# Scratch arrays of queries and keys laid out by plain rows instead of stacked blocks, in a hybrid encoder layer on one core

## The chip, the cores and the metric

The kernel runs on one core of a Trainium2 chip. The metric is the device time of one execution in microseconds (us), the median of several. In the profile PE is TensorE's matmuls, PEld its weight loads, DVE VectorE, ACT ScalarE, POOL GpSimd, SP SyncE, which here only issues DMAs; SPq and ACTq are the sequencers of SP and ACT, where a DMA's issue takes its time. L12 is line 12 of the kernel.

## The reference, cut to what matters

One encoder layer on x [2048, 1024], float32. Four token mixers read columns of one projection; the change touches the arrays of two of them, the differential attention (z_q, z_k) and the latent attention (from c_q, c_kv, k_r).

```python
a = rmsnorm(h, g_mix[i])
z = a @ w_in[i]
z_hy, z_s5, z_q, z_k, z_v, c_q, c_kv, k_r = split_mixer_columns(z)
y_hy = hyena_mixer(z_hy, ...); y_s5 = s5_mixer(z_s5, ...)
y_da = diff_attention(z_q..., z_k..., z_v..., lam, lam_init, da_g_head[i])   # 4 heads, 2 maps of 32
y_mla = mla_attention(c_q, c_kv, k_r, ...)     # 4 heads, 64 plain + 32 rotated; k_r shared by the heads
h = h + concatenate([norm(y_hy), norm(y_s5), y_da, norm(y_mla)]) @ w_out[i]
h = h + (silu(f @ w_gate[i]) * (f @ w_up[i])) @ w_down[i]      # f = rmsnorm(h)
h = h + sigmoid(rmsnorm(h) @ w_ple_gate[i]) * (p[i] @ w_ple[i])
return rmsnorm(h, g_final)
```

## The kernel before

Float32 products are made of fp32r ones: a number is split into hi + lo (`split`, `split_scaled`: ACT writes hi, DVE lo), and a product is three matmuls, hi hi, hi lo, lo hi (`mm3`, L52 to L54). The scores of attention do the same by stacking. For a differential map, 32 rows of a query's hi, hi, lo lie under each other on 96 partitions, against a key's hi, lo, hi, so that one matmul over 96 rows is the three products. For the latent attention, 64 plain rows and 32 rotated ones make 96, once for hi and once for lo, and a chunk of scores is three matmuls.

The stages, in the program's order:

1. *Input projection* (`InProj.run`), two halves of 1024 tokens. In each, groups of 256 or 304 columns: weights come by four loads (w_raw, L114, two places), are split, and products follow for two chunks of 512 tokens. Results go to scratch arrays in HBM. The columns of queries and keys pass through `to_stack` (L157): hi and lo tiles of [128, 512] (four blocks of 32 rows) are stored into S["qda"] and S["kda"], shaped [8, 96, 2048], hence each store names its target as 4 blocks x 32 rows x 512 tokens; one part is stored twice. These stores are issued on ACT's queue.
2. *Background.* Generators put their instructions between those of the foreground: first the Hyena filters, then `mla_prep`, which starts when the second half's latent columns are there; both must be through before attention. `mla_prep` runs over four chunks of 512 tokens: load c (L258), norm, rotate the shared key part, transpose (L291), project (L308), split into mp_hi and mp_lo (two places each), store to S["qml"] and S["kml"], shaped [4 heads, 2 parts, 96, 2048] (L319: 2 heads x 64 rows x 512; L331: 4 heads x 32 rows; L301: the rotated keys, the same rows for four heads, with the 32 rows outermost), then values: product, mp_v (one place), store of 128 rows (L339). Its PSUM tiles ps_hy have two places. All its DMAs, like the projection's weight loads, are on SP's queue, which issues in order.
3. *Attention* (`Attention`, `Unit`): per head 16 units of 128 queries, twelve chunks of scores each, the remaining background between them. Keys of a head are four tiles [96, 2048] with one place each (L368), asked for again when the last unit of a head has used them; a unit's queries are one tile [96, 4, 128] with two places, loaded by two DMAs (L409, L410).
4. Output projection, feed-forward part, gated embedding, final norm (L727 and on), which the change doesn't touch.

The order of instructions on each engine is set once, when the program is built, by a scheduler from the program's order and its priorities; on the chip each engine and each queue runs its list in order.

Of the kernel before, what the change touches and what calls it, by code (L numbers as in the profile page):

```python
# [24 lines left out]
class Ops:  # L25
    """Small helpers shared by the parts of the kernel."""
# [5 lines left out]
    def after(self, inst, earlier):  # L32
        """inst is issued after an earlier one of the same engine."""
        self.tc.add_manual_dep(inst.ins, earlier.ins.name, mybir.DependencyInfo(
            mybir.DependencyClass.NoSync, mybir.DependencyReason.DATA), reason="issue order")

    def split(self, hi, lo, src):
        """hi + lo == src exactly, each with 12 significant bits; src in SBUF or PSUM."""
        nc = self.nc
        nc.scalar.activation(hi, src, AF.Copy)  # L40
        nc.vector.tensor_sub(lo, src, hi.bitcast(F32))  # L41

    def split_scaled(self, hi, lo, src, scale):
        """The split of src * scale; scale is a number or one value per partition."""
        nc = self.nc
        nc.scalar.activation(hi, src, AF.Copy, scale=scale)
        nc.vector.scalar_tensor_tensor(lo, src, scale, hi.bitcast(F32), ALU.mult, ALU.subtract)

    def mm3(self, ps, lhs, rhs, first, last):
        """ps += lhs.T @ rhs, both given as (hi, lo)."""  # L50
# [5 lines left out]
    def rsqrt(self, y, v, t):  # L56
        """y = v ** -0.5 for v > 0, to float32's rounding; t is scratch. All [P, n]."""
# [8 lines left out]
def load_column(nc, dst, vec, n):  # L66
    """dst[p, c] = vec[c * 128 + p]"""
    nc.sync.dma_start(dst, vec.rearrange("(c p) -> p c", p=128))


class NormT:
    """Rows of a [SEQ, DM] stream -> rms norm -> transposed, scaled by g, split in two."""
# [5 lines left out]
    def chunk(self, rows, hi, lo, n=4, keep=False):  # L78
        """rows: n APs [128, DM] in SBUF, scaled in place unless kept; hi, lo: [128, 8, 128 n]."""
# [22 lines left out]
class InProj:  # L102
    """The columns of rmsnorm(x) @ w_in go to their scratch arrays."""
# [28 lines left out]
    def run(self, const, step, ready):  # L132
        """ready() comes when the latent attention's columns are there."""
        o, nc, A, S = self.o, self.nc, self.A, self.S
        with ExitStack() as ctx:
# [11 lines left out]
            def to_stack(dst, hi_rows, lo_row, scale):  # L147
                def done(ps, m, n0):
# [6 lines left out]
                    for src, rows in ((hi, hi_rows), (lo, (lo_row,))):  # L155
                        for r in rows:
                            nc.scalar.dma_start(dst[ds(4 * m, 4), ds(32 * r, 32), ds(n0, 512)], src.bitcast(F32))  # L157
                return done

            for half in range(2):  # L160
# [36 lines left out]
                columns_of((1024, to_stack(S["qda"], (0, 1), 2, qs)))  # L197
                columns_of((1280, to_stack(S["kda"], (0, 2), 1, None)))
# [10 lines left out]
                # chunk by chunk, so that the next half's first one finds a place early  # L209
# [15 lines left out]
def mla_prep(ops, const, A, S, cp, wk, ps_pool):  # L225
    """Queries, keys and values of the latent attention from the rows c_q | c_kv | k_rope.
    Queries carry minus the softmax scale; both come apart in two for the float32 products.
    A generator."""
# [26 lines left out]
    for ch in range(4):  # L255
# [44 lines left out]
        for j in range(2):  # L300
            nc.sync.dma_start(S["kml"][:, j, 64:96, ds(n0, 512)].rearrange("h d n -> d h n"),  # L301
                                a2[j][64:96].bitcast(F32)[:, None, :].to_broadcast([32, 4, 512]))
# [9 lines left out]
        for m in range(2):  # L312
            for dst, pairs, scale in ((S["qml"], q, MLA_SCALE), (S["kml"], ((wkv, kv),), 1.0)):
# [4 lines left out]
                for j, src in enumerate((hi, lo)):  # L318
                    nc.sync.dma_start(dst[ds(2 * m, 2), j, 0:64, ds(n0, 512)], src.bitcast(F32))  # L319
# [10 lines left out]
        for j, src in enumerate((hi, lo)):  # L330
            nc.sync.dma_start(S["qml"][:, j, 64:96, ds(n0, 512)], src.bitcast(F32))  # L331
# [11 lines left out]
class Attention:  # L343
    """Softmax attention over blocks of 128 queries, of a differential head (0) and a latent head (1) at a time.

    Scores lie as [query, key], with the sign changed, so that their least value is the maximum's
    negative; the weights are transposed on the tensor engine for the product with the values, and
    the sums' reciprocals scale the result."""

# [13 lines left out]
    def keys(self, i, h):  # L363
        """Two maps' keys of the differential head h, then two parts of the latent head's."""
        if h < 4:
            self.k[i] = self.kp.tile([96, SEQ], F32R, name=f"k{i}_sb")
            src = self.S["kda"][2 * h + i] if i < 2 else self.S["kml"][h, i - 2]
            self.nc.sync.dma_start(self.k[i].bitcast(F32), src)  # L368

    def values(self, i, h):  # L370
        """Half i of the keys' values."""
# [6 lines left out]
    def run(self, step):  # L378
        """One unit's chunks of scores at a time; after chunk k come the steps of PLAN[k], each of the unit so many
        units before."""  # L380
# [15 lines left out]
class Unit:  # L396
    """128 queries of two heads."""
# [6 lines left out]
    def chunk(self, k):  # L404
        at, nc, n = self.at, self.nc, self.t % 2
        if k == 0:
            tok = ds(128 * self.t, 128)
            self.q = at.qp.tile([96, 4, 128], F32R, name="q_sb")
            nc.sync.dma_start(self.q[:, 0:2].bitcast(F32), at.S["qda"][ds(2 * self.h, 2), :, tok].rearrange("m d n -> d m n"))  # L409
            nc.sync.dma_start(self.q[:, 2:4].bitcast(F32), at.S["qml"][self.h, :, :, tok].rearrange("j d n -> d j n"))  # L410
# [13 lines left out]
    def scores(self, name, c, products):  # L424
        """A chunk of scores, and of the last one the exponentials and their sum."""
# [20 lines left out]
    def combine(self):  # L446
        """The first map's weights less lambda times the second one's, times the first one's sum"""
# [15 lines left out]
    def scale(self, hd):  # L463
        """diag(1 / total)"""
# [20 lines left out]
    def weigh(self, piece):  # L485
        """The values' sums, by eight pieces of two chunks of keys, then times the queries' scales."""
# [25 lines left out]
def attention_consts(ops, cp, tmp, A):  # L512
    """strip[p, j] = |j - 1920 - p|, exact in 16 bits; neg_lam = minus the differential
    attention's lambda."""
# [20 lines left out]
def inverse_rms(ops, sm, rows, junk):  # L535
    """1 / the root mean square of each of some rows, a column each"""
# [9 lines left out]
class OutProj:  # L546
    """h = x + mix @ w_out with the branches' norms, and f = rmsnorm(h), transposed. The norms' gains go into w_out."""

    def __init__(self, st, const, A, S, cp):
# [11 lines left out]
        # columns that pick the two heads of 128 channels, or all of them  # L561
# [8 lines left out]
    def weights(self):  # L570
        """Forms the operands of w_out; those without a place yet go to scratch. A generator."""
# [9 lines left out]
    def fetch(self):  # L581
        """The operands that weights() put into scratch."""
# [5 lines left out]
    def prepare(self, t, wk, ps_pool):  # L588
        """mix of rows 256 t to 256 t + 255, transposed."""
# [6 lines left out]
        # mean squares: two branches' by row, four heads' and one branch's from their columns  # L596
# [17 lines left out]
        for m in range(2):  # L614
# [7 lines left out]
            # the columns' scales from diagonal matrices  # L622
# [14 lines left out]
    def run(self, wk, nwk, ps_pool, ps_norm):  # L637
        """Returns what is left to do: the last rows' norms."""
# [31 lines left out]
class Strassen:  # L670
    """C = A @ B by Winograd's seven products of blocks, A [256, K] and B [K, 1024] in 2 by 2 blocks:
    A11 B11, A12 B21, S4 B22, A22 T4, S1 T1, S2 T2, S3 T3 with S1 = A21 + A22, S2 = S1 - A11, S3 = A11 - A21,
    S4 = A12 - S2, T1 = B12 - B11, T2 = B22 - T1, T3 = B22 - B12 and T4 = B21 - T2 (its sign changed).
    Each product is one of float32 operands split in two."""
# [6 lines left out]
    def start(self, ctx):  # L681
        """The first pools, for four of B's operands and what they are formed from."""
# [5 lines left out]
    def complete(self, ctx):  # L688
        """The other pools, but those of raw() and sum()."""
        self.temporary.close()  # L690
        # what is needed first lies where attention's keys did, which are free before the rest
# [7 lines left out]
    def places(self, name, c, n=2):  # L699
        """An operand's tiles of chunks c and c + 1."""  # L700
# [7 lines left out]
    def forming(self, kb, load, scratch=None):  # L708
        """B's operands, with kb chunks of 128 rows in a block; load(tile, row of blocks, column, chunk) fills a
        tile with chunks from the given one on. The last three operands go to scratch, if given, by way of  # L710
        others' places. A generator."""
# [38 lines left out]
    def normed(self, dst, tok, h, g, const, wk, ps_pool, halves):  # L750
        """128 rows' norms times g, transposed; halves() gives the places of half of them as they are and transposed."""
# [14 lines left out]
    def halves(self):  # L766
        """Places for normed()."""
# [3 lines left out]
    def raw(self):  # L771
        """Tiles for two blocks of A, transposed: [row in a chunk, chunk, row of A]."""
        return [self.ar.tile([128, 4, 256], F32, name="a_raw") for _ in range(2)]

    def product(self, kb, raw, done):
        """done(row, column, terms) gets a block of C as the sum of terms, of which the first may lie in PSUM."""
# [49 lines left out]
    def sum(self, terms):  # L826
        """The sum, in SBUF or PSUM."""
# [10 lines left out]
def ffn(st, const, A, S, ctx, first):  # L838
    """h2 = h + (silu(f @ w_gate) * (f @ w_up)) @ w_down, from f transposed; first() follows the loads of the first
    half of f. Returns what is left to do: the norms of h2's last rows."""  # L840
    nc, last = st.nc, []
    # S["g"] = silu(f @ w_gate) * (f @ w_up), transposed
# [24 lines left out]
    # 6 or 8 chunks of the hidden columns at a time  # L867
# [40 lines left out]
def embedding(ops, const, A, S, cp, wk, ps_pool):  # L908
    """S["emb"] = p @ w_ple, 512 columns at a time. A generator."""
# [30 lines left out]
def ple(st, const, A, S, ctx, out, last):  # L940
    """out = rmsnorm(h2 + sigmoid(rmsnorm(h2) @ w_ple_gate) * emb); last is done first."""
# [46 lines left out]
def reduce_angle(nc, z, k):  # L988
    """z -= 2 pi * round(z / 2 pi), in place; k is scratch."""
# [8 lines left out]
class Dft16:  # L998
    """16-point complex transforms along the middle of z [128, 2 (re, im), 16, C], as two rounds of
# [826 lines left out]
```

## Time and profile before

| | us |
|---|---|
| runs | 4011.3, 4014.12, 4016.09; median 4014.12 |
| span of the profiled execution | 4006.2 |
| median less that span | 7.9 |
| TensorE busy over the span | 3526.0 (88%) |
| VectorE, ScalarE, GpSimd busy | 2700.0, 1801.4, 1863.9 |
| projection and preparation, until the first scores | 0 to 733.4 |
| attention, first to last score product | 733.4 to 2116.3 |

A busy share over the whole span mixes stages with different limits, so the stretches matter: in the page's 40 slices TensorE is busy seven to nine tenths and more in the last third, and five to six tenths in slices 5 to 8 (400 to 800 us). The profile keeps one time for the profiled execution, the span above; it is read beside the median.

### The profile page before, as it was taken

What the parts mean: (1) busy time and instruction counts of PE and PEld (TensorE: products, weight loads), DVE (VectorE), ACT (ScalarE), POOL (GpSimd) and SP (SyncE); (2) the same over time, 40 slices, a digit from 0 to 9 for tenths busy, and PEclk for the clock granted to TensorE, in tenths of its full rate; (3) what the DMA queues carried; (4) which work ended last, traced back from release to release, by engine and by line L of the source; (5) the groups of instructions that cost most, each with busy time, mean ns of one, the idle gap of its engine ahead of it and who ended that gap; (6) DMA issues with size and microseconds to landing.
All of it is one profiled execution on the core that took longest, in us unless ns stands there. A gap on an engine that the chain in (4) does not pass through costs nothing. (4 is left out here: it accounts for less than half of the span.)

```text
span 4006.2 us, 55513 instructions
## 1 busy us (share of the span) xinstructions
PE 3526.0 (88%) x19814; PEld 2806.2 (70%) x19814; DVE 2700.0 (67%) x5382; ACT 1801.4 (45%) x3089; POOL 1863.9 (47%) x1735
## 2 busy tenths in 40 slices
PE   8899656689999997877889879999999998989887
PEld 7789555466677775665667767888788876767666
DVE  6557322587776569888987786444845576768877
ACT  5224211366676765555565434333433343333344
POOL 1224000046419448767666655445544444344454
PEclk9999878799999998887998989999999999999988
DMA  4544432412442431241226453222322245544644
GB/s 144 177 140 163 141 112 87 108 50 82 152 153 82 130 132 54 74 130 41 62 82 216 137 158 118 84 82 84 107 88 74 85 138 172 178 168 153 206 153 156
DMA packets 349492, 486.18 MB, mean 121 GB/s; under 512 B 52987, under 2 KB 253439, under 8 KB 344703
## 3 DMA queue, kind: packets, MB, share of 16 engines
q1 hardware_dynamic: 273440, 370.69, 29.0%
q10 hardware_dynamic: 75776, 111.96, 8.0%
q8 instruction: 156, 2.56, 0.3%
q14 instruction: 120, 0.98, 0.1%
HBM read 313.46 MB, written 173.29 MB: 122 GB/s over the span
## 5 line engine op out<-in xcount | busy, mean ns | idle before, releaser
L434 PE MATMUL ps_s<-k_sb,q_sb 96*128 96x512 f32 x1280 | 474.8, 462 | 126.3 <-DVE four_s L439 52.7
L804 PE MATMUL ps_st<-t_hi,s_hi 128*128 128x512 f32 x984 | 398.3, 405 | 47.7 <-DVE st_sum L831 22.2
L444 ACT ACTIVATE at_s<-at_s,least_s 128x2048 f32<-128x2048 f32 x192 | 383.8, 2000 | 114.1 <-DVE least_s L443 88.8
L439 DVE CUSTOM_DVE_ANT_0 at_s<-ps_s,strip 128x512 f32<-128x512 f32 x512 | 339.3, 683 | 115.5 <-PE ps_s L434 89.6
L804 PE MATMUL ps_st<-t_hi,s_lo 128*128 128x512 f32 x984 | 393.5, 401 | 14.4 <-DVE s_lo L41 14.4
L804 PE MATMUL ps_st<-t_lo,s_hi 128*128 128x512 f32 x984 | 394.5, 401 | 12.5 <-DVE t_lo L41 12.5
L483 ACT ACTIVATE at<-ps_at 128x512 f32<-128x512 f32 x512 | 291.7, 593 | 246.4 <-PE ps_at L478 231.6
L434 PEld LDWEIGHTS ps_s<-k_sb,q_sb 96*128 96x128 f32 x1280 | 234.4, 201 | 216.0 <-DVE four_s L439 74.6
L40 ACT ACTIVATE s_hi<-s_raw 128x512 fp32r<-128x512 f32 (+1 forms) x336 | 207.5, 618 | 365.1 <-PE ps_st L804 285.9
L41 DVE TENSOR_TENSOR s_lo<-s_raw,s_hi 128x512 fp32r<-128x512 f32 (+1 forms) x336 | 269.4, 805 | 138.1 <-ACT s_hi L40 136.6
L478 PE MATMUL ps_at<-ident,at_s 128*128 128x128 f32 x2048 | 322.8, 291 | 30.2 <-ACT at L483 13.0
L488 PE MATMUL ps_o<-at,v_sb 128*64 128x128 f32 x4096 | 341.8, 291 | 7.7 <-DVE o_sb L505 5.3
L458 POOL TENSOR_SCALAR at_s<-at_s,f 128x1024 f32<-128x1024 f32 (+1 forms) x48 | 72.3, 1507 | 554.9 <-DVE f L452 503.5
L40 ACT ACTIVATE a_hi<-a_raw 128x512 fp32r<-128x512 f32 (+1 forms) x252 | 155.3, 618 | 386.7 <-PE ps_st L804 211.6
L488 PEld LDWEIGHTS ps_o<-at,v_sb 128*64 128x64 f32 x4096 | 248.5, 142 | 105.9 <-issue 89.5
L478 PEld LDWEIGHTS ps_at<-ident,at_s 128*128 128x128 f32 x2048 | 255.9, 149 | 88.9 <-issue 33.6
L788 POOL TENSOR_TENSOR s_raw<-a_raw 128x512 f32<-128x512 f32 (+1 forms) x84 | 111.4, 1326 | 425.2 <-DMA a_raw<-in_w_up_dram 129.7
L804 PE MATMUL ps_st<-b_hi,a_hi 128*128 128x512 f32 x656 | 264.7, 403 | 39.5 <-ACT b_hi L40 16.3
L41 DVE TENSOR_TENSOR a_lo<-a_raw,a_hi 128x512 fp32r<-128x512 f32 (+1 forms) x252 | 230.2, 916 | 70.2 <-ACT a_hi L40 69.1
L804 PE MATMUL ps_st<-b_lo,a_hi 128*128 128x512 f32 x656 | 262.5, 400 | 5.6 <-DVE b_lo L41 3.9
L804 PEld LDWEIGHTS ps_st<-t_hi,s_hi 128*128 128x128 f32 x984 | 191.0, 194 | 100.6 <-DVE st_sum L831 26.1
L804 PE MATMUL ps_st<-b_hi,a_lo 128*128 128x512 f32 x656 | 261.2, 398 | 0.0
(521 smaller groups left out, 8977.5 us busy)
## 6 DMA issues: line engine op xcount, KB each, us to landing
d_h<-st_row ACTq DMA_DIRECT2D x64, 512.0 KB
st_row<-d_h SPq DMA_DIRECT2D x64, 512.0 KB
a_raw<-in_w_gate_dram SPq DMA_DIRECT2D x44, 512.0 KB
a_raw<-in_w_up_dram SPq DMA_DIRECT2D x44, 512.0 KB
d_g<-st_row ACTq DMA_DIRECT2D x44, 512.0 KB
f_mat<-in_c_dft_f_dram SPq DMA_DIRECT2D x32, 512.0 KB
a_raw<-d_g SPq DMA_DIRECT2D x32, 512.0 KB
w_raw<-in_w_in_dram SPq DMA_DIRECT2D x48, 256.0 KB
```

The lines of the kernel that those rows point to most:

```text
L40: nc.scalar.activation(hi, src, AF.Copy)
L41: nc.vector.tensor_sub(lo, src, hi.bitcast(F32))
L434: nc.tensor.matmul(ps, lhsT=lhs, rhs=rhs[:, ts(c, 512)], start=n == 0, stop=n == len(products) - 1)
L439: nc.vector.tensor_tensor_reduce(dst, ps, at.strip[:, ds(1920 - 128 * self.t + 512 * c, 512)], self.slope, 3e38, ALU.add, ALU.min, least)
L444: nc.scalar.activation(s, s, AF.Exp, bias=least, scale=-1.0, accum_out=self.total[name])
L458: nc.gpsimd.tensor_scalar(s2[:, n:], s2[:, n:], f, 0.0, ALU.mult, ALU.add)
L478: nc.tensor.transpose(ps[:, j], src[:, ts(4 * g + j, 128)], at.ident)
L483: nc.scalar.activation(tile, ps, AF.Copy)
L488: mm = lambda out, lhsT, rhs, first, last: nc.tensor.matmul(out, lhsT=lhsT, rhs=rhs, start=first, stop=last, skip_group_check=True)
L788: eng.tensor_add(s1, a21, a22)
L804: nc.tensor.matmul(bank, lhsT=l[x][:, c], rhs=r[y], start=first and c + k == 0, stop=c == kb - 1 and k == 2, skip_group_check=True)
```

## The change

Scratch arrays hold the parts (hi, lo) apart, each as plain rows; a store is always one tile of 128 rows (32 for the rotated keys, stored once) by 512 tokens. The stacking moves to the loads: a map's key tile is loaded by three DMAs of 32 rows, a latent one by two (64 and 32 rows), a unit's queries by five. No engine's arithmetic changes. The new file also drops comments and docstrings. The core of the diff:

```diff
-            def to_stack(dst, hi_rows, lo_row, scale):
+            def to_parts(dst, scale):
...
-                    for src, rows in ((hi, hi_rows), (lo, (lo_row,))):
-                        for r in rows:
-                            nc.scalar.dma_start(dst[ds(4 * m, 4), ds(32 * r, 32), ds(n0, 512)], src.bitcast(F32))
+                    for j, src in enumerate((hi, lo)):
+                        nc.scalar.dma_start(dst[j, ts(m, 128), ds(n0, 512)], src.bitcast(F32))
...
-                columns_of((1024, to_stack(S["qda"], (0, 1), 2, qs)))
-                columns_of((1280, to_stack(S["kda"], (0, 2), 1, None)))
+                columns_of((1024, to_parts(S["qda"], qs)))
+                columns_of((1280, to_parts(S["kda"], None)))
...
-            nc.sync.dma_start(S["kml"][:, j, 64:96, ds(n0, 512)].rearrange("h d n -> d h n"),
-                                a2[j][64:96].bitcast(F32)[:, None, :].to_broadcast([32, 4, 512]))
+            nc.sync.dma_start(S["kmr"][j, :, ds(n0, 512)], a2[j][64:96].bitcast(F32))
...
-                    nc.sync.dma_start(dst[ds(2 * m, 2), j, 0:64, ds(n0, 512)], src.bitcast(F32))
+                    nc.sync.dma_start(dst[j, ts(m, 128), ds(n0, 512)], src.bitcast(F32))
...
-            nc.sync.dma_start(S["qml"][:, j, 64:96, ds(n0, 512)], src.bitcast(F32))
+            nc.sync.dma_start(S["qmr"][j, :, ds(n0, 512)], src.bitcast(F32))
...
-            src = self.S["kda"][2 * h + i] if i < 2 else self.S["kml"][h, i - 2]
-            self.nc.sync.dma_start(self.k[i].bitcast(F32), src)
+            k, S = self.k[i].bitcast(F32), self.S
+            if i < 2:
+                for r, part in enumerate((0, 1, 0)):
+                    self.nc.sync.dma_start(k[ts(r, 32)], S["kda"][part, ts(2 * h + i, 32)])
+            else:
+                self.nc.sync.dma_start(k[0:64], S["kmn"][i - 2, ts(h, 64)])
+                self.nc.sync.dma_start(k[64:96], S["kmr"][i - 2])
+
+    def queries(self, h, t):
+        S, tok = self.S, ts(t, 128)
+        tile = self.qp.tile([96, 4, 128], F32R, name="q_sb")
+        q = tile.bitcast(F32)
+        for r, part in enumerate((0, 0, 1)):
+            self.nc.sync.dma_start(q[ts(r, 32), 0:2], S["qda"][part, ts(h, 64), tok].rearrange("(m d) n -> d m n", m=2))
+        self.nc.sync.dma_start(q[0:64, 2:4], S["qmn"][:, ts(h, 64), tok].rearrange("j d n -> d j n"))
+        self.nc.sync.dma_start(q[64:96, 2:4], S["qmr"][:, ts(h, 32), tok].rearrange("j d n -> d j n"))
+        return tile
...
-            tok = ds(128 * self.t, 128)
-            self.q = at.qp.tile([96, 4, 128], F32R, name="q_sb")
-            nc.sync.dma_start(self.q[:, 0:2].bitcast(F32), at.S["qda"][ds(2 * self.h, 2), :, tok].rearrange("m d n -> d m n"))
-            nc.sync.dma_start(self.q[:, 2:4].bitcast(F32), at.S["qml"][self.h, :, :, tok].rearrange("j d n -> d j n"))
+            self.q = at.queries(self.h, self.t)
...
-    for name, shape in (("qda", [8, 96, SEQ]), ("kda", [8, 96, SEQ]), ("qml", [4, 2, 96, SEQ]),
-                        ("kml", [4, 2, 96, SEQ]), ("b_out", [3, 2, 128, 4, 512])):
+    for name, shape in (("qda", [2, 256, SEQ]), ("kda", [2, 256, SEQ]), ("qmn", [2, 256, SEQ]), ("qmr", [2, 128, SEQ]),
+                        ("kmn", [2, 256, SEQ]), ("kmr", [2, 32, SEQ]), ("b_out", [3, 2, 128, 4, 512])):
```

## Rows read from the trace of the kernel before

**Rows 1.** Stretches: length; busy us of PE, PEld, DVE, ACT, POOL; PEclk; DMA; GB/s.

```profile
175.00:200.00 25.00, 14.02 (x81) 13.71 (x80) 8.48 (x22) 2.79 (x5) 0.00 (x0) 0.69 0.49 172
400.00:425.00 25.00, 25.00 (x116) 20.88 (x115) 7.65 (x14) 3.79 (x7) 6.89 (x8) 1.00 0.61 196
425.00:733.00 308.00, 176.95 (x775) 144.72 (x773) 80.78 (x223) 46.18 (x121) 0.00 (x0) 0.78 0.32 106
625.00:650.00 25.00, 17.98 (x70) 13.72 (x69) 3.75 (x6) 2.39 (x4) 0.00 (x0) 0.91 0.18 62
```

**Rows 2.** Waits of TensorE, 430 to 750 us: us in total, times, longest.

```profile
PE ps_hy L52 <- DVE mp_lo L47: 63.3, 9, 13.5
PE ps_hy L52 <- DVE mp_v L338: 34.9, 3, 15.1
PE ps_s L434 <- DMA k_sb<-d_kml: 11.8, 1, 11.8
PE ps_s L434 <- DMA k_sb<-d_kda: 9.2, 1, 9.2
```

**Rows 3.** Waits of all engines on DMAs, 425 to 750 us.

```profile
DVE mp_v L338 <- DMA d_vml<-mp_v: 59.2, 9, 18.5
ACT w_hi L40 <- DMA w_raw<-in_w_in_dram: 41.6, 4, 20.9
DVE mp_lo L47 <- DMA d_qml<-mp_lo: 39.6, 4, 15.3
```

**Rows 4.** Timeline of SP's queue: start us, us to issue, queue, line, DMA.

```profile
627.08 0.53 SPq L319 DMA_DIRECT2D d_qml<-mp_hi  x1
...
653.22 5.61 SPq L319 DMA_DIRECT2D d_kml<-mp_lo  x1
...
717.06 4.90 SPq L368 DMA_DIRECT2D k_sb<-d_kda  x1
...
729.62 7.86 SPq L368 DMA_DIRECT2D k_sb<-d_kml  x2
...
1734.53 0.32 SPq L409 DMA_DIRECT2D q_sb<-d_qda  x1
```

**Rows 5.** Issues that write d_kml: ns min/median/max, first and last start.

```profile
L319 SPq DMA_DIRECT2D d_kml<-mp_hi x8: 515/1537/6511, 474.1 to 722.1; - x8
...
L301 SPq DMA_DIRECT2D d_kml<-cq_hi x4: 318/326/453, 453.7 to 689.2; - x4
```

**Rows 6.** Issues that read the tile z_ev: the store of 128 plain rows.

```profile
L205 ACTq DMA_DIRECT2D d_zhyT<-z_ev x24: 326/326/327, 238.7 to 714.4; - x24
```

**Rows 7.** Timeline of TensorE at the full clock: start us, busy us, instruction.

```profile
170.22 0.27 PE L52 MATMUL ps_ip<-w_hi,aT_hi 128*128 128x256 f32 x1
...
174.89 0.28 PE L52 MATMUL ps_ip<-w_hi,aT_hi 128*128 128x256 f32 x1
...
420.17 0.39 PE L52 MATMUL ps_ip<-aT_hi,w_hi 128*128 128x512 f32 x1
...
432.41 0.39 PE L52 MATMUL ps_ip<-aT_hi,w_hi 128*128 128x512 f32 x1
```

**Rows 8.** Groups of TensorE, 432 to 752 us: busy us, mean ns, idle.

```profile
L52 PE MATMUL ps_ip<-aT_hi,w_hi 128*128 128x512 f32 x115 | 47.5, 413 | 0.0
...
L52 PE MATMUL ps_ip<-w_hi,aT_hi 128*128 128x256 f32 x64 | 20.3, 317 | 0.0
L52 PE MATMUL ps_hy<-cq_hi,wq_hi 128*128 128x512 f32 (+1 forms) x32 | 17.7, 554 | 56.9 <-DVE mp_lo L47 56.9
```

**Rows 9.** The chain of waits, pieces of the feed-forward part: start us, us, what.

```profile
3339.32 5.54 DMA d_h<-st_row
...
3502.48 3.58 DMA d_h<-st_row
```

**Rows 10.** Instructions on the tile q_sb: the score products, first and last start.

```profile
L434 PE MATMUL ps_s<-k_sb,q_sb x1280: 387/473/797, 733.4 to 2116.3; 96*128 96x512 f32 x183
```

**Rows 11.** Timeline of TensorE, 1740 to 1775 us: a unit's first products.

```profile
1760.99 1.25 PE L434 MATMUL ps_s<-k_sb,q_sb 96*128 96x512 f32 x3
```

More of the change, by code (lines that the diff above doesn't have):

```diff
@@ L312, in mla_prep @@
         for m in range(2):
-            for dst, pairs, scale in ((S["qml"], q, MLA_SCALE), (S["kml"], ((wkv, kv),), 1.0)):
+            for dst, pairs, scale in ((S["qmn"], q, MLA_SCALE), (S["kmn"], ((wkv, kv),), 1.0)):
                 ps = project(m, pairs)
```

## The prediction

> **What bounds the kernel now.** I read the busy time by stretch first, because the change touches three places only: the second half of the input projection with the latent attention's preparation beside it, the start of attention, and the loads of attention. Up to 425 us the tensor engine is the limit: in 400 to 425 us it is busy all the time at the full granted clock. Then come 308 us in which it is busy 177, the clock is 0.78, vector and scalar engines are busy 81 and 46, GpSimd not at all, and the DMA engines 0.32 [rows 1]. No engine is the limit there by its mean, so the waits have to say what is.
>
> The tensor engine's waits from 430 to 750 us sum to 143.7 us. The largest are for mp_lo (63.3, nine times) and mp_v (34.9 + 2.6), the evacuations of the preparation's products, and for the keys (11.8 + 9.2) [rows 2]; six smaller rows of that answer are the other 24.5 with the 2.6. One step further back, mp_lo and mp_hi wait for the stores d_qml and d_kml two before them, whose tiles they write again, mp_v for its own store of 128 rows, and the foreground's weights for loads that name none of the changed arrays (41.6 us in four waits, the longest 20.9) [rows 3]. All these go through SP's queue.
>
> That queue is what the reader should look at. From 627.08 to 653.22 + 5.61 = 658.83 us SP issues eight stores of 256 KB back to back: 31.75 us, 3.97 each [rows 4], 66 GB/s. In a stretch inside it (625 to 650) the DMA engines are busy 0.18, at 62 GB/s; in 400 to 425 they were busy 0.61 at 196 [rows 1]. A queue that is full while 0.18 x 16 = 2.9 engines are busy is waiting for a few engines, not for bandwidth. Which form does that is seen in the issue times. The store with 64 rows by two heads (outermost length 2) takes 515 ns at the least and 6511 at the most; the one with 32 rows outermost 318 to 453 [rows 5]; a plain store of 128 rows of the same 256 KB 326 to 327 in all its 24 issues [rows 6]. So I read: a store whose outermost dimension is 2 or 4 goes to two or four DMA engines, and everything behind it on the queue waits, the weights, the values' stores and the keys included.
>
> The Trainium skill says the same as a rule ("DMA: Bandwidth & Descriptors", section "Why a DMA increments its semaphore by 16 and not by 1"): a DMA uses the largest number of engines up to 16 that divides the outermost non-unit sizes of both sides. With its figure of about 27 GiB/s for an engine, half of 256 KB on each of two engines would take 4.5 us, an estimate, against the 3.97 of the trace, so it agrees; 32 such stores would give back some 125 us of SP's time, and the sum by that would be 3889 us.
>
> **The change, part by part.** *Stores of the preparation.* 32 stores with outermost length 2 and 8 with 4 become 128 plain rows, the form of rows 6. Their issue falls to 0.33 us; their landing I take as 3.5 us, between nothing and the 3.58 and 5.54 us that stores of 512 KB show in the chain [rows 9], nearer the lower since they are half as large. What the tensor engine needs of its own in 432 to 752 us: at the warm pace 54 products of 512 columns take 432.41 - 420.17 = 12.24 us, 0.2267 each, and 39 of 256 columns 174.89 - 170.22 = 4.67 us, 0.1197 each [rows 7]. The stretch holds 3 x 115 projection products of 512 columns (78.2 us), 3 x 64 of 256 (23.0), 3 x 32 for queries [rows 8] and 3 x 8 for keys (27.2), and 104 small ones (45 for values, 48 transposes, 11 scores: 5.4 + 5.7 + 2.5). That is 142. So 320 us = 142 of work + 144 of waits + 34 that the lower clock and overlap cost.
>
> Of the waits, mp_lo's 63.3 shrink to some 10: twenty evacuations with two places each, where the store two back has 0.33 + 3.5 us to land and two projections of six products (2.7 us) with the foreground's products between cover nearly all. That is -53 (ends: -30 if covers are poor, -63). mp_v keeps its one place: four stores in a row per chunk, of which the tensor engine, two PSUM places ahead, feels about two: 4 x (2 x 3.5 - 3 of foreground work) = 16, so 37.5 falls to 16: -21 (ends 0 and -37). mp_r's and the other small ones (24.5 less the 2.6 of mp_v = 22) were partly behind the same queue: -4 (ends 0, -10). The lost clock follows the waits: of 34 us I give back 19 (ends 8 and 34).
>
> *Keys' first load.* Issued at 717.06, with the latent ones issued from 729.62 among the last stores and taking 7.86 us to issue [rows 4]; the tensor engine stood still 21.0 us for them. Four tiles of 768 KB at the 196 GB/s of rows 1 need 16 us, part of it beside the first scores: 21 to 12, -9 (ends 0, -15). The ten pieces in place of four cost 6 x 0.32 us of issue, beside that.
>
> *Input projection.* Each block's hi (or lo) part was stored twice, in 4 rows-of-32 blocks: 48 stores on ACT's queue become 32 plain ones. Half lie before 430 us, where the tensor engine is already full but for one hole: 175 to 200 us, busy 14.02 of 25 [rows 1], during which the scalar engine's weights wait for d_kda. I take 8 of these 11 us back (ends 0, -11).
>
> *Shared rotated keys.* Stored once rather than for four heads: 1.5 MB less, with 32 rows outermost before and after; only bytes, and at 0.32 busy they cost nothing.
>
> *Loads in attention.* A unit's queries come by five DMAs rather than two, a head's keys by ten rather than four: 64 x 3 + 4 x 6 = 216 more on SP. Runs of 512 B and 8 KB stay as they were, and all pieces have 32 or 64 rows outermost. At 0.32 us [rows 4] that is 69 us of SP, in a stage of 1383 us [rows 10]; queries are asked for when a slot falls free, at 1734.53 for the unit whose products start at 1760.99 [rows 4, 11]: 26 us of cover for 1 us more of issue, behind which SP's other loads wait 1 us longer. If the cover were gone, 64 x 1.0 us. I take +3 for the three head changes, where the latent keys are needed soonest, and for extra waits of the tensor engine on a tile with several writers (ends 0 and +20, one piece's issue uncovered in each of 64 units).
>
> The Trainium skill speaks against this part ("DMA: Bandwidth & Descriptors", "Rules for kernel authors"): small transfers should be joined, since below 64 KB the overhead is most of it, and disjoint halves of the partitions should go in one transfer; a query piece is now 32 to 64 KB instead of 96. With the page's fixed 2 us for each of 192 more it would be 384 us if none were covered, an estimate; the cover of 26 us for each unit speaks against it.
>
> Sum: -53 - 21 - 4 - 19 - 9 - 8 + 3 = -111. The profiled execution's span is 4006.2 us, and the median of the runs 4014.12, 7.9 more; so 4006.2 - 111 = 3895 profiled, **3903** as timed. Everything after 750 us keeps its order and moves forward.
>
> **Rivals.** (1) *The next limit is close.* Stores land fast, but single places (mp_v, the rotation's r1, the transposed operands) and two PSUM places chain the preparation, so that only the waits that name the changed stores go: half of mp_lo's (32), with 8 of clock, 8 of the hole and 4 of keys: 52 less, 3962. For it: mp_v's wait is on a store that does not change form. Against: those stores wait behind the changed ones, on the same queue, which the weights' loads do too [rows 3].
>
> (2) *The number of engines does not depend on the form.* Then only bytes count: of 24 stores of the second half 8 go, 2 MB, 32 us at 66 GB/s, and 1.5 MB of rotated keys, 8 us at 196 GB/s. Waits are 144 of the stage's 320 us, 0.45, so 18 of these 40 are felt: 3996. Against it stand rows 5 and 6.
>
> (3) *Slower: the loads of attention.* If each unit waited for its extra query pieces by more than 111 / 64 = 1.75 us, the gain would be gone; at 2.5 us, a landing less the issue that overlaps, it is +160, giving 4014 - 114 + 160 = 4060. It needs the 26 us of cover to vanish, which no row shows: in the view of the queries' tile no load of queries is named as the tensor engine's wait.
>
> (4) *All waits go:* 144 of waits but 12 of keys and 13 of the small ones, 34 of clock, 11 of the hole: some 164 less, 3850.
>
> **How the numbers follow.** All lower ends at once are -18 (3996), all upper ones -170 (3844); they hardly meet, and the forecast's own range is -75 to -150 (3864 to 3939). It gets 0.66; rival 1 0.18; rival 4 0.07; rival 2 0.05; rival 3 0.04. The range 3850 to 3965 holds the forecast, most of rival 1 and half of rival 4, 0.83. Within 0.2% (8 us, about what a measurement of this kernel can tell from no change) lies part of rival 2, 0.02; slower by more, rival 3 and what a shifted order elsewhere could cost, 0.05; faster 0.93.
>
> **What would show it.** Right: no issue of a changed store above some 1 us; the tensor engine's busy share between 430 us and the first scores above 0.75 with a clock above 0.9; the first scores at 610 to 650 us instead of 733; mp_v the largest wait left; attention as long as before (733 to 2116 us) within 10 us. Wrong: SP's issues still of several microseconds; or attention longer, with query or key loads named before score products; or a stage just as long with waits on PSUM places in place of those on stores.

## The result, and the profile after

The changed kernel takes 3855.7 us (median of four runs, 3846.66 to 3857.39), the kernel before 4014.57 beside it; the ratio is 0.9602 (95% interval 0.9588 to 0.9615). That is 159 us less. The forecast was 3903 in a range of 3850 to 3965, faster with 0.93. The profiled execution, the fastest of the four, has a span of 3844.9 us, 161.3 less than the 4006.2 of before.

The stretches (same columns as [rows 1]): the hole at 175 to 200 us, the stage up to the first scores, and the start of attention.

```profile
175.00:200.00 25.00, 25.00 (x220) 25.00 (x219) 17.54 (x46) 4.79 (x19) 0.00 (x0) 1.00 0.58 179
425.00:558.00 133.00, 130.08 (x690) 110.49 (x688) 60.35 (x146) 31.05 (x74) 0.00 (x0) 1.00 0.54 177
550.00:575.00 25.00, 14.44 (x49) 9.81 (x48) 11.43 (x28) 4.04 (x6) 0.00 (x0) 0.74 1.00 262
```

The stage that took 425 to 733 us with TensorE busy 177 of 308 at a granted clock of 0.78 [rows 1] ends at 558, busy 130 of 133 us at the full clock. The hole at 175 is closed. What follows it is new: from 550 to 575 the DMA engines are busy all the time, at 262 GB/s, and TensorE 14 of 25 us. The loads of the first keys and values and the last stores of the preparation are issued in these 25 us.

TensorE's waits from 425 to 640 us (columns as in [rows 2]):

```profile
PE ps_s L447 <- DMA k_sb<-d_kmr: 6.9, 2, 6.3
...
PE ps_hy L52 <- DVE mp_lo L47: 2.3, 2, 1.5
...
PE ps_hy L52 <- DVE mp_v L336: 1.4, 2, 0.8
...
PE ps_s L447 <- DMA k_sb<-d_kda: 0.2, 1, 0.2
```

mp_lo and mp_v, 63.3 and 34.9 us before [rows 2], are 2.3 and 1.4. The keys lead the list now. The foreground's waits for its weight loads, 41.6 us from 425 to 750 us before [rows 3], are 6.4 from 425 to 558.

SP's timeline has the same eight stores of one chunk that [rows 4] shows back to back; the first and the last of them:

```profile
503.89 0.34 SPq L317 DMA_DIRECT2D d_qmn<-mp_hi  x1
...
516.52 0.32 SPq L317 DMA_DIRECT2D d_kmn<-mp_lo  x1
```

They are not back to back any more: there are gaps between them, and each issue takes 0.32 to 0.34 us; before, there was one every 3.97 us. All issues that write the latent keys (columns as in [rows 5]):

```profile
L317 SPq DMA_DIRECT2D d_kmn<-mp_hi x8: 319/322/782, 434.3 to 553.2; - x8
L317 SPq DMA_DIRECT2D d_kmn<-mp_lo x8: 319/320/443, 435.1 to 556.4; - x8
```

The least is 319 ns, near that of a plain store, where it was 515 [rows 5]. Of all the stores that changed, one takes long, one of the rotated queries' at 565.1 us with 5.22 us, inside the 25 us in which the DMA engines are full. The store of 128 plain rows that does not change (columns as in [rows 6]) shows how far ahead the projection is; its first issue moved from 238.7 us to 222.5:

```profile
L204 ACTq DMA_DIRECT2D d_zhyT<-z_ev x24: 326/326/355, 222.5 to 551.5; - x24
```

And attention, first and last score product of the queries' tile, with the loads named in TensorE's waits on it over the whole run (us, times):

```profile
L447 PE MATMUL ps_s<-k_sb,q_sb x1280: 387/476/797, 558.3 to 1970.5; 96*128 96x512 f32 x183
...
  DMA k_sb<-d_kmr: 9.7, 5
  DMA k_sb<-d_kmn: 6.1, 1
...
  DMA q_sb<-d_qda: 0.8, 1
```

Attention runs from 558.3 to 1970.5 us, 1412 long; before it was 733.4 to 2116.3 [rows 10], 1383. So the 161.3 us of the span are 175.1 up to the first scores, less 29.3 that attention grew, plus 15.5 that the rest after the last score became shorter (1889.9 to 1874.4; in the thirteen kernels below this rest is 1871 to 1891 us, so the 15.5 cannot be put down to the change).

The two stretches of attention:

```profile
733.00:2116.00 1383.00, 1221.85 (x9025) 921.22 (x9026) 1091.99 (x2701) 867.80 (x1379) 818.72 (x866) 0.93 0.31 95
558.00:1970.00 1412.00, 1244.30 (x9025) 931.40 (x9024) 1091.28 (x2706) 871.34 (x1382) 843.40 (x870) 0.92 0.32 96
```

The same 9025 products take TensorE 1244.3 us (second row) in place of 1221.9 (first row, before): 22.4 of the 29 us are slower products, at a mean granted clock of 0.92 against 0.93, and 6.6 are idle time.

### The profile page after: what moved, and what is told of

Its sections match the earlier page's. It is cut to its first block, busy times and chain, and to the rows that moved or that the text cites. A ratio compares the mean times of both kernels' runs of the same rounds, so it can differ in the third digit from the quotient of the medians.

```text
span 3844.9 us, 55782 instructions
## 1 busy us (share of the span) xinstructions
PE 3504.9 (91%) x19814; PEld 2782.5 (72%) x19814; DVE 2678.9 (70%) x5382; ACT 1802.5 (47%) x3089; POOL 1869.3 (49%) x1735
## 5 line engine op out<-in xcount | busy, mean ns | idle before, releaser
L447 PE MATMUL ps_s<-k_sb,q_sb 96*128 96x512 f32 x1280 | 483.9, 466 | 109.9 <-DVE four_s L452 51.1
L501 PE MATMUL ps_o<-at,v_sb 128*64 128x128 f32 x4096 | 352.9, 296 | 11.2 <-DVE o_sb L518 4.8
L501 PEld LDWEIGHTS ps_o<-at,v_sb 128*64 128x64 f32 x4096 | 256.8, 145 | 111.5 <-issue 91.7
```

The costliest lines, as they stand in the source:

```text
L447: nc.tensor.matmul(ps, lhsT=lhs, rhs=rhs[:, ts(c, 512)], start=n == 0, stop=n == len(products) - 1)
L501: mm = lambda out, lhsT, rhs, first, last: nc.tensor.matmul(out, lhsT=lhsT, rhs=rhs, start=first, stop=last, skip_group_check=True)
```

## The experiments

All kernels in one view; attention is first to last score product of the profiled execution, and the ratio is to the kernel before on the same chip, with its 95% interval.

| kernel | first score | attention | median us | ratio |
|---|---|---|---|---|
| before | 733.4 | 1383 | 4014.57 | 1 |
| changed | 558.3 | 1412 | 3855.70 | 0.9602 (0.9588 to 0.9615) |
| wide stores, old arrays | 580.8 | 1416 | 3886.28 | 0.9691 (0.9676 to 0.9705) |
| narrow stores, new arrays | 711.9 | 1412 | 4011.10 | 1.0008 (0.9999 to 1.0018) |
| split loads, old stores | 746.4 | 1402 | 4036.65 | 1.0069 (1.0054 to 1.0084) |
| latent part alone | 621.5 | 1419 | 3929.62 | 0.9806 (0.9791 to 0.9821) |
| differential part alone | 668.5 | 1422 | 3972.75 | 0.9898 (0.9880 to 0.9916) |
| gaps, but 16 blocks | 560.4 | 1406 | 3850.19 | 0.9601 (0.9587 to 0.9616) |
| before, other pace | 737.0 | 1394 | 4006.71 | 0.9989 (0.9979 to 0.9999) |
| changed, pace up | 563.1 | 1441 | 3882.28 | 0.9679 (0.9659 to 0.9698) |
| changed, pace down | 559.2 | 1436 | 3873.85 | 0.9657 (0.9643 to 0.9672) |
| changed, third pace | 561.6 | 1411 | 3861.68 | 0.9626 (0.9609 to 0.9643) |
| changed, loads doubled | 562.3 | 1423 | 3877.00 | 0.9667 (0.9652 to 0.9682) |

The theory: a store with 2 or 4 blocks outermost (a narrow store, below) goes to few DMA engines and blocks the queue for everything behind it; the new arrays make rows outermost (a wide store), and that is the gain. The rivals: the bytes stored twice; the gaps between the blocks; and, for what attention lost, the cut loads against a new order of instructions.

**Wide stores with the old arrays.** Only the stores are cut by blocks; arrays, doubled stores and loads are those of before.

```diff
-    nc.scalar.dma_start(dst[ds(4 * m, 4), ds(32 * r, 32), ds(n0, 512)], src.bitcast(F32))
+    for b in range(4):
+        nc.scalar.dma_start(dst[4 * m + b, ds(32 * r, 32), ds(n0, 512)], src[ts(b, 32)].bitcast(F32))
...
-    nc.sync.dma_start(dst[ds(2 * m, 2), j, 0:64, ds(n0, 512)], src.bitcast(F32))
+    for b in range(2):
+        nc.sync.dma_start(dst[2 * m + b, j, 0:64, ds(n0, 512)], src[ts(b, 64)].bitcast(F32))
...
-    nc.sync.dma_start(S["qml"][:, j, 64:96, ds(n0, 512)], src.bitcast(F32))
+    for b in range(4):
+        nc.sync.dma_start(S["qml"][b, j, 64:96, ds(n0, 512)], src[ts(b, 32)].bitcast(F32))
```

> The kernel before, with its arrays, its doubled stores and its two query loads and four key loads; only each store of stacked blocks is cut by blocks: four stores of 32 rows (differential, rotated queries) or two of 64 rows (latent), so that rows are outermost in every store. Theory, the form of the stores decides through the number of DMA engines: first scores near 560 us and a time near the changed kernel's, 3840 to 3870, as wide stores are all there is to gain. Rival, bytes: nothing is stored less, so no gain from that, 3990 to 4015. Rival, the loads of attention cost what attention grew (1383 to 1412 us from first to last score): with the old loads 3815 to 3840. Rival, the single-engine price of issuing: ACT issues 192 stores in place of 48, some 45 us more of its queue; if that reached the projection, 3890.

3886 us, 123 less than before: three quarters of the gain without a new array, 16 us above the theory's range and beside the 3890 of the rival that counts the issues on ACT's queue. The stretch before its first scores:

```profile
425.00:581.00 156.00, 137.66 (x717) 116.08 (x715) 71.23 (x182) 36.40 (x82) 0.00 (x0) 0.95 0.69 193
```

TensorE is busy 138 of 156 us, the clock 0.95 and the DMA share 0.69 where the changed kernel has 0.54. The profiled span is 38.6 us longer than the changed kernel's, and 22.5 of that stand before the first scores, with many more stores on the queues (192 against 32 on ACT's) and some rows still stored twice. Which of the two it is, no run tells. Attention is as long as in the changed kernel with the loads of before, which is a first mark against the cut loads.

**Narrow stores with the new arrays.** The changed kernel, its stores, loads and bytes; the arrays only have unused rows between blocks, so that a store has 2 or 4 blocks outermost.

```diff
-    nc.scalar.dma_start(dst[j, ts(m, 128), ds(n0, 512)], src.bitcast(F32))
+    nc.scalar.dma_start(dst[j, ds(4 * m, 4), 0:32, ds(n0, 512)], src.bitcast(F32))
...
-    nc.sync.dma_start(dst[j, ts(m, 128), ds(n0, 512)], src.bitcast(F32))
+    nc.sync.dma_start(dst[j, ds(2 * m, 2), 0:64, ds(n0, 512)], src.bitcast(F32))
...
-    ("qda", [2, 256, SEQ]), ("kda", [2, 256, SEQ]), ("qmn", [2, 256, SEQ]), ("qmr", [2, 128, SEQ])
+    ("qda", [2, 8, 48, SEQ]), ("kda", [2, 8, 48, SEQ]), ("qmn", [2, 4, 96, SEQ]), ("qmr", [2, 4, 48, SEQ])
```

> The changed kernel, with its numbers of stores and loads, its shared rows stored once and its five query loads and ten key loads; only the scratch arrays have unused rows between the blocks, so that a store again has 2 or 4 blocks outermost. Theory, the form of the stores decides: the queue is blocked again, issues of several us return, first scores near 730 us, time 3985 to 4030. Rival, bytes stored decide: as the changed kernel, 3845 to 3875. Rival, part of the gain is from storing less on ACT's queue: in between, 3930 to 3980.

The whole gain in time is gone: 1.0008. Its issues that write the latent keys, TensorE's waits from 425 to 730 us, and the stretch up to its first scores:

```profile
L317 SPq DMA_DIRECT2D d_kmn<-mp_hi x8: 491/1552/4954, 476.9 to 700.7; - x8
L317 SPq DMA_DIRECT2D d_kmn<-mp_lo x8: 1445/4340/5592, 477.5 to 701.3; - x8
```

```profile
PE ps_hy L52 <- DVE mp_lo L47: 59.8, 9, 14.2
PE ps_hy L52 <- DVE mp_v L336: 55.3, 4, 14.4
```

```profile
425.00:712.00 287.00, 166.68 (x753) 136.60 (x751) 77.32 (x213) 41.74 (x103) 0.00 (x0) 0.78 0.29 94
```

Issues of up to 5.6 us, waits on mp_lo and mp_v, clock 0.78 and a DMA share of 0.29 are back, as in [rows 1], [rows 2] and [rows 5]. The bytes are those of the changed kernel, so they are not the gain. The first scores do come 21.5 us earlier than before (711.9 against 733.4, and the theory said near 730), of the change's 175.1; attention, 28.6 us longer than before, takes that back. Whether the 21.5 are the bytes' or a new order's, no run tells.

**Gaps, but 16 blocks.** That run changed two things at once, the outermost length and the gaps. Here the plain latent rows lie in blocks of 8 with 4 unused rows behind each: more gaps, but 16 blocks outermost.

```diff
-    nc.sync.dma_start(dst[j, ts(m, 128), ds(n0, 512)], src.bitcast(F32))
+    nc.sync.dma_start(dst[j, ts(m, 16), 0:8, ds(n0, 512)], src.bitcast(F32))
...
-    self.nc.sync.dma_start(k[0:64], S["kmn"][i - 2, ts(h, 64)])
+    self.nc.sync.dma_start(k[0:64], S["kmn"][i - 2, ts(h, 8), 0:8])
...
-    self.nc.sync.dma_start(q[0:64, 2:4], S["qmn"][:, ts(h, 64), tok].rearrange("j d n -> d j n"))
+    for j in range(2):
+        self.nc.sync.dma_start(q[0:64, 2 + j], S["qmn"][j, ts(h, 8), 0:8, tok])
...
-    ("qmn", [2, 256, SEQ]) ... ("kmn", [2, 256, SEQ])
+    ("qmn", [2, 32, 12, SEQ]) ... ("kmn", [2, 32, 12, SEQ])
```

> The changed kernel, with the plain rows of the latent queries and keys in 16 blocks of 8 rows for each store, 4 rows unused behind each, so that a store again jumps between separate places but has 16 blocks outermost instead of 2; the loads of these rows have 8 blocks outermost, and a unit's latent queries come by one load more. Theory, the number of DMA engines set by the outermost length decides: issues of these stores stay under 1 us, first scores at 555 to 575 us, time 3850 to 3885 (keys' loads with 8 outermost may cost some us at four heads). Rival, the gaps between blocks make the stores slow: issues of several us, first scores above 650 us, 3920 to 4010.

As fast as the changed kernel. The issues that write the latent keys, and the stretch up to the first scores:

```profile
L317 SPq DMA_DIRECT2D d_kmn<-mp_hi x8: 517/522/1187, 434.3 to 556.4; - x8
L317 SPq DMA_DIRECT2D d_kmn<-mp_lo x8: 518/518/557, 435.6 to 557.1; - x8
```

```profile
425.00:560.00 135.00, 130.35 (x692) 110.87 (x690) 61.14 (x147) 31.27 (x74) 0.00 (x0) 1.00 0.56 172
```

A store in 16 separate places takes 0.52 us to issue, more than the 0.32 of a plain one, but at most 1.24 us, and the stage is full at the full clock. It is the outermost length and not the gaps (tried here for the plain latent rows alone).

How many engines the stores keep busy can be read where SP's queue, q1, has nothing but them: packets, MB, share of 16 engines, of the kernel before from 642 to 652 us, of the narrow stores with the new arrays from 622 to 632, and of this run from 519 to 521, while two stores land.

```profile
q1 hardware_dynamic: 254, 0.51, 13.1%
q1 hardware_dynamic: 253, 0.51, 13.1%
q1 hardware_dynamic: 246, 0.47, 81.3%
```

13.1% of 16 is 2.1 engines, for ten microseconds on end, with a full queue; 81.3% is 13.0. By the rule of the Trainium skill ("DMA: Bandwidth & Descriptors", section "Why a DMA increments its semaphore by 16 and not by 1"), 2 blocks would use 2 engines and 16 blocks 16; these rows agree with it.

**Each half alone.** The changed kernel with the differential arrays, stores and loads of before, and the complement.

```diff
-    columns_of((1024, to_parts(S["qda"], qs)))
-    columns_of((1280, to_parts(S["kda"], None)))
+    columns_of((1024, to_stack(S["qda"], (0, 1), 2, qs)))
+    columns_of((1280, to_stack(S["kda"], (0, 2), 1, None)))
```

```diff
-    for dst, pairs, scale in ((S["qmn"], q, MLA_SCALE), (S["kmn"], ((wkv, kv),), 1.0)):
+    for dst, pairs, scale in ((S["qml"], q, MLA_SCALE), (S["kml"], ((wkv, kv),), 1.0)):
...
-    nc.sync.dma_start(dst[j, ts(m, 128), ds(n0, 512)], src.bitcast(F32))
+    nc.sync.dma_start(dst[ds(2 * m, 2), j, 0:64, ds(n0, 512)], src.bitcast(F32))
```

> The change for the latent attention's arrays alone; queries and keys of the differential attention keep the stacked arrays, the doubled stores of 4 blocks of 32 rows on ACT's queue and their whole loads. Theory, the stores with 2 blocks outermost on SP's queue are most of it: SP's long issues go, the hole at 175 to 200 us stays and the differential stores crowd four engines at 425 to 500 us: first scores at 580 to 620 us, time 3875 to 3925. Rival, both halves are needed, as either fills the same few engines: 3930 to 3990. Rival, the differential stores never mattered: 3850 to 3870.

> The complement of the run on the latent part alone: the differential attention's arrays as changed, the latent ones as before, with 2 or 4 blocks outermost on SP's queue. Theory, SP's queue of narrow stores is what holds the stage: SP's issues of several us stay, first scores at 690 to 725 us, time 3965 to 4005. Rival, the two halves add up to the whole (80 us came from the latent part, 156 from both): 3925 to 3945. Rival, either half alone frees the few engines enough: below 3920.

The latent part alone gives 80 us, 4.6 above the theory's range and at the lower end (3930) of the rival's that both halves are needed; the differential part alone gives 39 us, inside its range, though its first scores come at 668.5 us and not at 690 to 725. Together they would be 119, and the change gives 159. Each half's narrow stores hold the queue that issues them: with the differential part alone SP's issues of latent keys still take up to 6.1 us, with the latent part alone ACT's of differential queries up to 4.3. Why the whole is worth 40 us more than its halves, no run shows. The stretches of the latent part alone, then of the differential part alone:

```profile
175.00:200.00 25.00, 10.66 (x78) 10.28 (x76) 10.28 (x24) 4.10 (x9) 0.00 (x0) 0.80 0.48 167
425.00:621.00 196.00, 161.98 (x798) 137.02 (x796) 81.25 (x223) 46.42 (x121) 0.00 (x0) 0.91 0.49 164
```

```profile
175.00:200.00 25.00, 24.85 (x214) 24.50 (x213) 17.36 (x46) 5.08 (x19) 0.00 (x0) 1.00 0.57 182
425.00:669.00 244.00, 155.66 (x701) 128.05 (x701) 62.22 (x154) 31.98 (x75) 0.00 (x0) 0.80 0.32 102
```

The hole at 175 us belongs to the differential stores (10.7 of 25 busy with them narrow, 24.9 with them wide; 18.8 in the run of narrow stores with the new arrays, where no row is stored twice), the long stage more to the latent ones (clock 0.80 and share 0.32 with them narrow, 0.91 and 0.49 with them wide).

**Split loads with the old stores.** What attention grew by (29 us) is tried by itself: the kernel before, with the loads cut as in the change.

```diff
-    self.nc.sync.dma_start(self.k[i].bitcast(F32), src)
+    for r in range(3):
+        self.nc.sync.dma_start(k[ts(r, 32)], src[ts(r, 32)])
...
-    nc.sync.dma_start(self.q[:, 0:2].bitcast(F32), at.S["qda"][ds(2 * self.h, 2), :, tok].rearrange("m d n -> d m n"))
+    for r in range(3):
+        nc.sync.dma_start(q[ts(r, 32), 0:2], at.S["qda"][ds(2 * self.h, 2), ts(r, 32), tok].rearrange("m d n -> d m n"))
```

(The latent tiles are cut in 64 and 32 rows in the same way.)

> The kernel before, with its stores and arrays; only the loads of attention are cut as in the change, five for a unit's queries and ten for a head's keys. Theory, loads are covered: within 8 us of before, 4006 to 4022, attention 1383 us within 10. Rival, the cut loads cost what attention grew, 29 us: 4035 to 4050, with longer waits on loads of keys or queries. Rival, it was the order that the scheduler chose anew: anything up to 30 us either way, without loads named in the waits.

27 us slower: the theory's time was wrong, and the time of the rival for the cut loads was met, though not its longer waits. The score products and the loads of keys in TensorE's waits on the queries' tile read:

```profile
L443 PE MATMUL ps_s<-k_sb,q_sb x1280: 387/477/797, 746.4 to 2148.1; 96*128 96x512 f32 x183
...
  DMA k_sb<-d_kml: 17.5, 6
```

But of the 22.4 us by which its profiled span is longer, 13 had been lost before the first score (746.4 against 733.4), with the same stores as before, and attention grew by 19, not 29, while the named waits for keys were 17.5 us in all against 23.3 before (14.1 for latent ones, 9.2 for differential ones). The time alone doesn't tell the loads from the order; the next runs take it up.

**The order of instructions.** One number of the background's pace is changed, which moves its instructions among those of attention, in the kernel before and three times in the changed one; and the loads are cut once more.

```diff
-RATES = [5.0, 8.0, 1.2, 1.2, 1.0, 2.0]
+RATES = [5.0, 8.0, 1.2, 1.3, 1.0, 2.0]
```

(The pace down has 1.1 in that place; the third pace has 1.1 in place of 1.0.)

> The kernel before with one number of the background's pace changed, 1.2 to 1.3 for the state-space and embedding part, which touches no store and no load of queries or keys; it only moves instructions of the background among those of attention. Theory, the attention of the kernel before (1383 us) came by a lucky order and any new order costs about 30 us: attention 1395 to 1425 us, time 4020 to 4045. Rival, the loads cut in pieces cost the 29 us, and order is worth little: attention 1373 to 1393, time 4000 to 4020.

> The changed kernel with the same number changed, 1.2 to 1.3. Theory, order: attention anywhere in 1385 to 1430 us, time 3830 to 3875, the difference to 3856 made within attention. Rival, loads cost the 29 us: attention within 10 us of 1412.

> The changed kernel with that number changed the other way, 1.2 to 1.1. Theory, order: attention anywhere in 1385 to 1430 us, time 3830 to 3875. Rival, loads: attention within 10 us of 1412.

> The changed kernel with the pace of the Hyena part 1.0 to 1.1, a third sample of the order. Theory, order: attention 1385 to 1441 us, 3830 to 3890. Rival, loads: within 10 us of 1412.

> The changed kernel with its loads of attention cut once more: ten for a unit's queries in place of five, twenty for a head's keys in place of ten, with the same bytes. Theory, the loads are covered and the growth of attention (1383 to 1412 us) is the order's: attention 1395 to 1441 us, the span of the runs at other paces, and the waits named for queries or keys below 30 us in all; time 3845 to 3885. Rival, the loads cost it (29 us for 216 more of them, so some 45 to 55 for 344 more): attention 1455 to 1475, 3895 to 3915, with waits on queries.

For the loads doubled, a differential key tile comes in pieces of 16 rows and a query piece for each map or part by itself:

```diff
-    self.nc.sync.dma_start(k[ts(r, 32)], S["kda"][part, ts(2 * h + i, 32)])
+    for x in range(2):
+        self.nc.sync.dma_start(k[ds(32 * r + 16 * x, 16)], S["kda"][part, ds(64 * h + 32 * i + 16 * x, 16)])
```

The kernel before did not lose by the other pace: attention 11 us longer (1394, between the theory's 1395 and the rival's 1393), the whole 4 us shorter, as the rival had it. That part of the theory (any new order costs 30 us) fell. The changed kernel has 1441, 1436 and 1411 us by the pace alone. The first two are above the theory's 1430 and outside the rival's 1402 to 1422; the third fits both; the first has a time 7 us above the theory's range. The pace up:

```profile
L447 PE MATMUL ps_s<-k_sb,q_sb x1280: 387/476/797, 563.1 to 2004.5; 96*128 96x512 f32 x183
```

And with 360 more loads (320 of queries and 40 of keys; the 344 of the expectation was a miscount) it has 1423, less than two of these, with 17.2 + 8.5 + 3.4 us of named waits for keys:

```profile
L451 PE MATMUL ps_s<-k_sb,q_sb x1280: 387/475/797, 562.3 to 1984.9; 96*128 96x512 f32 x183
...
  DMA k_sb<-d_kmr: 17.2, 5
  DMA k_sb<-d_kmn: 8.5, 1
  DMA k_sb<-d_kda: 3.4, 1
```

The rival's 1455 to 1475 for doubled loads did not come. So the order moves attention by 30 us without any change in loads, and with twice the loads it is 11 us longer, where the keys' waits are 13 us longer (29.1 against 15.8). What stays open: every kernel with the cut loads or an early start has attention of 1402 to 1441 us, the two with whole loads and a late start 1383 and 1394. No run separates the loads' small share from the order's, since every change of the loads also makes a new order.

## Why the prediction was right, and what was mis-sized

*What bounds the stage.* Right: the two runs that set the outermost length, down to 2 or 4 and up to 16, put the first scores at 711.9 and at 560.4 us, against 733.4 before and 558.3 changed, and SP's queue keeps 2.1 engines busy with 2 blocks. [rows 4 to 6] had pointed to it, though their ranges were read from one of two rows each: the other part's stores (lo) took up to 8.8 us with 2 blocks, and up to 0.89 with 32 rows outermost. The prediction's second mechanism, that everything behind on the queue waits too, shows in mp_v, whose store kept its form and whose wait went from 37.5 to 1.4 us, and in the weight loads (41.6 to 6.4).

*The size.* The forecast's own range (3864 to 3939) was missed; the time came out beside rival 4, all waits go (3850), which had a chance of 0.07. The mis-sized term is "Of the waits": the waits that were to stay in it. mp_lo was to keep 10 us and kept 2.3; mp_v was to keep 16 and kept 1.4; of the 22 of the small ones 18 were to stay, and the preparation's (mp_r, cq_lo, ckv_lo and one put down to issue) are all gone from the list; of the 34 us of clock 15 were to stay, and the clock is 1.00. Summed over these four groups that is 61 + 36 + 22 + 34 = 153 us instead of 97. The landing of 3.5 us was about right: in the changed kernel the stores of the plain latent rows take 2.1 to 3.6 us in the middle from issue to landing. Rather, I had costed the preparation as a chain by itself and had put too little of the projection's products between its steps: in the changed kernel 130 busy us fill 133. That this is the reason is argued, not tried. So rival 1, the next limit is close, did not come: the waits on single places and PSUM are 3.7 us in all (mp_lo and mp_v).

*Luck.* Of its signs the issue times (but for one of 5.22 us) and the full, fast stage came; the first scores came 52 us before the 610 to 650, the keys and not mp_v are the largest wait left, and attention grew. That the time lies inside the stated range, 5.7 us above its lower end, is in part luck: had attention grown by the +3 of the sum and the rest stayed as it was, it would have been 3855.7 - 26.3 + 15.5 = 3845, an estimate from the spans, below the range. Two errors of opposite sign met, a stage that gained more than the sum had and an attention that lost.

*The projection.* 8 us were given back for the hole, 16.2 came (238.7 to 222.5 at the first plain store). The hole was 11 us of idle time; the sum left out that the products beside it ran at a granted clock of 0.69, and at 0.96 in the next 25 us, where the changed kernel has 1.00.

*The keys.* Predicted 21 to 12; at the start 7.1 are left, and 8.9 more come later in attention. While the first were waited for, the DMA engines were busy 1.00.

*The loads of attention.* +3 predicted (ends 0 and 20), attention grew by 29. The mechanism that I priced is nearly absent: waits for queries 0.8 us, for keys 15.8 in all against 23.3 in the same view of before. What I put at nothing is that TensorE's order in attention would change: "Everything after 750 us keeps its order" is wrong, and by the pace alone attention is 1411 to 1441 us. That the order is what cost the 29 us is likely and not shown. Rival 3 (slower by 64 waits) is excluded by the doubled loads: 10 for a unit, named waits for queries of 2.5 us, and a time 21 us above the changed kernel's, inside what pace alone does (3856 to 3882). The Trainium skill ("DMA: Bandwidth & Descriptors", section "Rules for kernel authors") has small transfers joined into large ones; not doing so has no price here that stands out from the order's.

*Rival 2*, bytes: excluded as the cause by the narrow stores with the new arrays, which store what the change stores and are at 1.0008. There the first scores come 21.5 us earlier than before, near the 18 that the rival gave the bytes; that these 21.5 are the bytes' is not shown.

## What to carry to other kernels

When a DMA queue's issues take microseconds while the DMA engines are mostly idle, look at the outermost length of the stores in it, on the side of HBM too: 2 or 4 blocks of rows held up here everything behind them (2.1 of 16 engines busy, a store every 3.97 us), and cutting the store by blocks was worth 123 us without a new layout. Price such a stall by the work that is left when all of its waits are gone, not only by those waits that name the store: the victims were a store that did not change, weight loads and the clock. And a change of the number of DMAs can give a scheduler another order: a pace that touches no store and no load moved this kernel by up to 27 us.

## What the runs showed of the hardware that I had not expected

A store of 256 KB in 16 separate places takes 0.52 us to issue against 0.32 in one (and about 0.5 at the least with 2), yet the kernel is as fast: the longer issue is not the harm, the full queue is. After the stage was mended the DMA engines are full from 550 to 575 us, a share of 1.00 at 262 GB/s, where the highest share in [rows 1] was 0.61. It is not the bytes alone: from 425 to 450 us the changed kernel moves 258 GB/s at a share of 0.81. In the full stretch 3454 of 5234 packets are under 512 B, in the other 397 of 4649; that the small packets are the reason was not tried.
